# Queries set in halves by transfers, sums added by transfers, reciprocals for two blocks: one hybrid attention block on one core

## The chip, the cores and the metric

One core of a Trainium2 chip runs the whole kernel. Times are device microseconds (us) of one execution. TensorE (PE) multiplies, and its weight loads are listed apart (PEld). VectorE (DVE), ScalarE (ACT) and GpSimd (POOL) work on tiles of 128 partitions. SyncE (SP) and POOL issue transfers (DMAs); a transfer issued by POOL can add what it carries to what is there ("accumulating").

## What is computed

The reference is a decoder block on 16 meta tokens and 512 positions, 1024 channels, all in float32. Cut to what matters here:

```python
proj = h @ w_in                      # h: layer norm of the input; 10 groups of 1024 columns
q_d, k_d, v_d, g_d, q_s, k_s, v_s, g_s, m_d, m_s = split(proj)
# 8 differential heads, two softmaxes each:
s = q @ k.T * 64 ** -0.5 - slope * distance
a = softmax(s0) - lam * softmax(s1);  y_d = rms_norm(a @ v) * 0.8
# 16 stick-breaking heads of 64:
z = q @ k.T * 64 ** -0.5
a = exp(log_sigmoid(z) + sum of log_sigmoid(-z) over later keys);  y_s = a @ v
br_d = (y_d * silu(g_d)) @ w_br_diff;  br_s = (y_s * silu(g_s)) @ w_br_sb
y = (sigmoid(m_d + b) * br_d + sigmoid(m_s + b) * br_s) @ w_out
out = layer_norm(2 ** 0.25 * h + y)
```

## The kernel before, in words

Precision: an operand x of a product is split into a rounded part xh and the rest xl = x - xh, and a product is made of three, xh·yh, xh·yl and xl·yh. Every weight tile (128 x 512) therefore goes through two instructions: ACT rounds it (`hi`, line 174), DVE subtracts (`lo`, line 179).

Order: the work is 16 units (line 69), eight differential heads "d" and eight pairs of stick-breaking heads "s". While unit u's scores and values are worked out, TensorE projects the keys and values of unit u+1 and the queries of unit u+2, and, in "s" units, the two gates. `run` (line 532) mixes the projections with steps that are due at given times. This is the program's order; in the middle section, over all units, the build plans the order on each engine from it, with a model of the durations. `placed` (line 213) ties one instruction behind the one before it on its engine; `keep_order` fixes the order of the start and of the part after the units.

Weights: `items` (line 86) lists the roundings in order, `loads` the transfers that feed them. `fetch` (line 126) asks for a load as soon as a buffer of its ring is free (six "raw", four "rawk", four "rawa"); `prep` (line 183) rounds one item four items ahead of its use. For the eight "s" units keys and values of both halves of the positions are made by seven quarter-size products in place of eight (`stage_kv`, line 633). Of each unit's seven weight operands some are sums of quarters of the weights. a21+a11 and a21+a22 are made by an accumulating transfer from POOL on top of a plain load (`added`, line 148), and two further sums by DVE (`add`, line 153) into a tile `sum`.

Queries (`stage_q`, line 569; the first two heads in `q_hi` and `q_lo`, lines 337 and 341): the projection leaves two heads of 64 rows in one bank. For each head c a tile A[c] holds the rounded query in the head's own 64 partitions and the rest in the other 64. This takes two ACT and two DVE instructions on 64 partitions each:

```python
s.activation(A[c][own], ps[own], AF.Copy, scale=0.125)
v.scalar_tensor_tensor(A[c][oth], ps[own], 0.125, A[c][own], op0=ALU.mult, op1=ALU.subtract)
```

The keys K[c] (line 565) are laid out to match and filled by transfers on SP (`store_k`, line 601).

Differential scores (`d_scores`, line 775) go over four blocks of 128 queries, largest first. After each block's exponentials DVE takes the two reciprocals (line 808), multiplies one by -lambda (809) and combines the two softmaxes (810, 811). The values' sum of squares is split by ACT and POOL (`sqh`, `sql`, line 834) for a product with ones (`ms`, line 841).

Stick-breaking values (`s_values`, line 876): two 64-row halves of a bank `av` must be added. ACT copies one half to `half` (line 889), DVE adds it to the other (line 890) into `ys`. `half` shares one buffer with two tiles of the differential heads. POOL multiplies `ys` by the gate (line 516), and SP stores it (line 518).

Of the kernel before, what the change touches and what calls it, by code (L numbers as in the profile page):

```python
# [16 lines left out]
P = 128  # L17
# [27 lines left out]
def hybrid_block_kernel(ctx: ExitStack, tc: tile.TileContext, x, meta, emb_g, emb_b, w_in, b_gate,  # L45
# [71 lines left out]
    rings = {"raw": (6, []), "rawk": (4, []), "rawa": (4, [])}  # L117
# [8 lines left out]
    def fetch(most=99):  # L126

        for order in (sum_loads, other_loads):
            while order and most:
                l = order[0]  # L130
                src, more, tag = loads[l]
                bufs, log = rings[tag]
                if len(log) >= bufs and left[log[-bufs]] or tag not in pools:
                    break
                raw = pools[tag].tile([P, 4, P], F32, tag=tag, name=tag, bufs=bufs)
                nc.sync.dma_start(raw if l < WOUT else raw.rearrange("p a b -> p (a b)"), src)
                if more is not None:
                    second[l] = lambda raw=raw, more=more: g.dma_start(raw, more, accum_op=ALU.add)
                    if tag == "rawa":
                        added(l)  # L140
                    else:
                        later.append((state["n"] + 3, lambda l=l: added(l)))
                        later.sort(key=lambda x: x[0])
                raws[l] = raw
                log.append(order.pop(0))
                most -= 1

    def added(l):

        if l in second:  # L150
            placed(second.pop(l), ORDERED[3:])
# [14 lines left out]
    def hi(h):  # L166
# [3 lines left out]
        added(item)  # L170
# [165 lines left out]

    def q_hi(n):
        for c, own, _ in HEADS:
            s.activation(A0[n][c][own], pss[n][own], AF.Copy, scale=0.125)

    def q_lo(n):
        for c, own, oth in HEADS:
            a = A0[n][c]
            v.scalar_tensor_tensor(a[oth], pss[n][own], 0.125, a[own].bitcast(F32), op0=ALU.mult, op1=ALU.subtract)
# [199 lines left out]
    with tc.tile_pool(name="att", bufs=1) as ap:  # L544
        pools["sum"] = ap
# [20 lines left out]
        for c, own, oth in HEADS:  # L566
            g.memset(K[c][oth, 1, :].bitcast(F32), 0.0)

        def stage_q(unit, kind, n):
# [12 lines left out]
        def stage_k(unit, kind, n, direct=False):  # L582
# [3 lines left out]
            for m in range(2):  # L586
# [3 lines left out]
                if direct:  # L590
                    for c, own, oth in HEADS:
                        s.copy(K[c][own, 0, o], ps[own])
                        v.tensor_tensor(K[c][own, 1, o], ps[own], K[c][own, 0, o].bitcast(F32), op=ALU.subtract)
                        s.copy(K[c][oth, 0, o], ps[own])
# [6 lines left out]
        def store_k():  # L601

            for o, t in staged:
                for c, own, oth in HEADS:
                    nc.sync.dma_start(K[c][own, :, o].bitcast(F32), t[own].bitcast(F32))
                    nc.sync.dma_start(K[c][oth, 0, o].bitcast(F32), t[own, 0].bitcast(F32))
# [168 lines left out]
        def d_scores(unit, h):  # L775
# [15 lines left out]
            for i in reversed(range(NB)):  # L791
# [15 lines left out]
                r = rz[:, i, :]  # L807
                v.reciprocal(r, zs[:, i, :])
                v.tensor_scalar(r[:, 1:2], r[:, 1:2], nlam, None, op0=ALU.mult)
                v.tensor_scalar(e[0], e[0], r[:, 0:1], None, op0=ALU.mult)  # L810
                v.scalar_tensor_tensor(a[:, AOFF[i]:AOFF[i] + nk], e[1], r[:, 1:2], e[0], op0=ALU.mult, op1=ALU.add)
# [64 lines left out]
        def s_values(unit, c, p, ta):  # L876
# [13 lines left out]
            v.tensor_tensor(unit["y"][own], av[own], half[own], op=ALU.add)  # L890
# [82 lines left out]
    pools["rawa"] = pools["sum"] = lp  # L973
# [228 lines left out]
```

## Time and profile before

| what | value |
|---|---|
| median of three runs | 727.53 us (727.27 to 727.58) |
| the profiled execution | 728.81 us |
| its span, first to last instruction | 727.0 us |
| mean granted TensorE clock | 0.996 |
| instructions | 13330 |

In the profile "a<-b" means that tile a is written from tile b, "x16" counts instructions, and "L890" is line 890 of the kernel. A row of a wait names who waited, for whom, and the total, the count and the longest in us. In a timeline the bracket is the engine's idle time ahead of the instruction and who ended it.

### The profile page before, as it was taken

The page shows a single profiled execution, that of the slowest core. Times are in us where ns is not written, and L with a number is a line of the kernel's source. Part 1 is how long each engine was busy: PE and PEld are TensorE (multiplying, and loading weights), DVE is VectorE, ACT ScalarE, POOL GpSimd, SP SyncE. Part 2 cuts the span into 40 slices and gives each one's busy share as a digit, 9 for nine tenths or more (in the row PEclk, how much of TensorE's full clock was granted, in tenths as well). Part 3 has the DMA queues.
Part 4 walks back from the last instruction along what each step waited for, and adds up shares of the span by engine and source line. Part 5 has one row for each costly group of instructions (what it writes and reads, how often), then busy time and mean ns, then how long its engine had stood idle before and what let it go on. Part 6 is the DMA issues. An engine that isn't in the chain of part 4 may idle for free.

```text
span 727.0 us, 13330 instructions
## 1 busy us (share of the span) xinstructions
PE 713.1 (98%) x4594; PEld 649.6 (89%) x4594; DVE 585.6 (81%) x1246; ACT 428.8 (59%) x1023; POOL 111.7 (15%) x133
## 2 busy tenths in 40 slices
PE   9999999999999999999999999999999999999994
PEld 8999999999999888898989898988888998999783
DVE  6887668678998889797968797968395888778787
ACT  5675666666787776575756575655365455555300
POOL 3210141011012000130202000001012202130002
PEclk9999999999999999999999999999999999999998
DMA  8343448343346644647645443583258748696802
GB/s 292 97 140 101 126 121 146 101 133 102 109 102 149 156 132 124 152 106 185 139 139 130 121 119 102 177 259 102 59 143 162 146 119 184 137 182 189 302 20 101
DMA packets 153798, 101.86 MB, mean 140 GB/s; under 512 B 7249, under 2 KB 141810, under 8 KB 153730
## 3 DMA queue, kind: packets, MB, share of 16 engines
q1 hardware_dynamic: 135650, 89.99, 42.6%
q0 software_dynamic: 17760, 9.96, 10.7%
q10 hardware_dynamic: 320, 1.06, 0.4%
q8 instruction: 36, 0.59, 0.3%
q14 instruction: 32, 0.26, 0.1%
HBM read 79.38 MB, written 7.86 MB: 120 GB/s over the span
## 4 chain that ended last, share of the span: by engine, by line
PE 82%; DMA 6%; DVE 6%; ACT 3%; issue 1%; POOL 1%; SPq 0%; DVEq 0%; POOLq 0%; ACTq 0%
PE ps L500 12%; PE ps L484 11%; PE ps L486 11%; PE ps L485 11%; PE q L1009 10%; PE q L651 10%; PE sc L717 5%; PE t L723 3%; DMA raw<-in_w_out_dram 2%; PE t L728 1%; PE bank L375 1%; DMA ysT<-gs 1%; PE av L885 1%; PE tv L684 1%; PE av L886 1%
## 5 line engine op out<-in xcount | busy, mean ns | idle before, releaser
L179 DVE TENSOR_TENSOR wl<-raw,wh 128x512 fp32r<-128x512 f32 x172 | 119.0, 697 | 34.6 <-ACT wh L174 33.0
L485 PE MATMUL ps<-hTl,wh 128*128 128x512 f32 x368 | 145.6, 396 | 0.0
L484 PE MATMUL ps<-hTh,wh 128*128 128x512 f32 x368 | 145.3, 395 | 0.2 <-DVE kvt L668 0.2
L486 PE MATMUL ps<-hTh,wl 128*128 128x512 f32 x368 | 144.5, 393 | 0.0
L174 ACT CAST wh<-raw 128x512 fp32r<-128x512 f32 x172 | 105.5, 622 | 34.0 <-PE ps L485 20.2
L486 PEld LDWEIGHTS ps<-hTh,wl 128*128 128x128 f32 x368 | 69.2, 188 | 13.5
L484 PEld LDWEIGHTS ps<-hTh,wh 128*128 128x128 f32 x368 | 69.2, 188 | 13.2 <-DVE kvt L668 0.4
L485 PEld LDWEIGHTS ps<-hTl,wh 128*128 128x128 f32 x368 | 69.2, 188 | 12.4
L500 PE MATMUL ps<-hTh,wh 128*128 128x264 f32 x256 | 73.5, 287 | 0.0
L500 PE MATMUL ps<-hTl,wh 128*128 128x264 f32 x256 | 73.4, 287 | 0.0
L500 PE MATMUL ps<-hTh,wl 128*128 128x264 f32 x256 | 73.2, 286 | 0.0
L717 PE MATMUL sc<-k,A 128*128 128x264 f32 (+3 forms) x320 | 66.6, 297 | 0.5 <-DMA k<-ks 0.3
L734 DVE TENSOR_TENSOR al<-t,ah 128x512 fp32r<-128x512 f32 (+2 forms) x88 | 45.6, 526 | 25.2 <-ACT ah L733 19.4
L1009 PE MATMUL q<-gh,wl 128*128 128x256 f32 x224 | 63.8, 285 | 0.0
L1009 PE MATMUL q<-gl,wh 128*128 128x256 f32 x224 | 63.6, 284 | 0.0
L1009 PE MATMUL q<-gh,wh 128*128 128x256 f32 x224 | 63.1, 282 | 0.2 <-ACT t L1018 0.2
L733 ACT CAST ah<-t 128x512 fp32r<-128x512 f32 (+2 forms) x88 | 40.2, 465 | 34.5 <-PE t L723 26.3
L871 DVE TENSOR_TENSOR_SCAN e<-e,diag 128x528 f32<-128x528 f32 (+1 forms) x64 | 54.6, 858 | 4.9 <-ACT e L865 4.6
L717 PEld LDWEIGHTS sc<-k,A 128*128 128x128 f32 x320 | 50.4, 189 | 4.1 <-issue 0.7
L500 PEld LDWEIGHTS ps<-hTh,wl 128*128 128x128 f32 x256 | 48.3, 189 | 0.5
L500 PEld LDWEIGHTS ps<-hTl,wh 128*128 128x128 f32 x256 | 48.3, 189 | 0.5
L500 PEld LDWEIGHTS ps<-hTh,wh 128*128 128x128 f32 x256 | 48.3, 188 | 0.4
(274 smaller groups left out, 1764.6 us busy)
## 6 DMA issues: line engine op xcount, KB each, us to landing
raw<-in_w_in_dram SPq DMA_DIRECT2D x144, 256.0 KB, 3.2
k<-ks SPq DMA_DIRECT2D x60, 132.0 KB, 2.7
rawk<-in_w_in_dram SPq DMA_DIRECT2D x16, 256.0 KB, 3.4
rawk<-in_w_in_dram POOLq DMA_DIRECT2D x16, 256.0 KB, 6.5
raw<-in_w_out_dram SPq DMA_DIRECT2D x16, 256.0 KB, 3.5
k<-ks SPq DMA_DIRECT2D x60, 66.0 KB, 2.3
raw<-in_w_br_diff_dram SPq DMA_DIRECT2D x12, 256.0 KB, 3.7
raw<-in_w_br_sb_dram SPq DMA_DIRECT2D x12, 256.0 KB, 3.5
```

The costliest lines, as they stand in the source:

```text
L174: s.copy(wh, raw)
L179: eng.tensor_tensor(wl, raw, wh.bitcast(F32), op=ALU.subtract)
L484: pe.matmul(ps, wh[:, k % 4, :], hTh[:, k, M:], start=(k == 0), stop=False)
L485: pe.matmul(ps, wh[:, k % 4, :], hTl[:, k, M:], start=False, stop=False)
L486: pe.matmul(ps, wl[:, k % 4, :], hTh[:, k, M:], start=False, stop=(k == KT - 1))
L500: pe.matmul(ps[:, :H2], a[:, k % 4, :], b[:, k, ts(c, H2)], start=(k == 0 and m == 0), stop=(k == KT - 1 and m == 2))
L651: pe.matmul(bank, a[:, k, :], b, start=start and k == 0 and j == 0, stop=k == 3 and j == 2, skip_group_check=not start)
L717: pe.matmul(ps[:, :n], q, K[:, m, k0:k0 + n], start=(m == 0), stop=(m == 1))
L733: s.copy(h, t[:, o:o + w])
L734: v.tensor_tensor(l, t[:, o:o + w], h.bitcast(F32), op=ALU.subtract)
L871: v.tensor_tensor_scan(rev, rev, diag[0][:, L - nk:][:, ::-1], 0.0, ALU.mult, ALU.max)
L1009: pe.matmul(bank, a[:, k, :], b[:, n, k, :], start=start and k == 0 and m == 0, stop=k == 3 and m == 2, skip_group_check=not start)
```

## The change

- `stage_q`: ACT rounds both heads at once on 128 partitions into A[0], DVE subtracts both at once into a new tile `low`, and three transfers on SP set the halves in their places. `q_hi` and `q_lo` keep two instructions each, with other partitions. The rest now stands in partitions 64 to 127 for both heads, and the keys' layout follows.
- Weights of the "s" units: the sum a21+a22+a11 is loaded once and added to twice by transfers; a21+a22 gets a load and an accumulation of its own. One DVE addition per unit stays, made in place. The ring "rawk" has five buffers, and the tile `sum` of the middle section goes.
- `d_scores`: reciprocals, the multiplication by -lambda and the combination are made for two blocks after every second block.
- `s_values`: ACT copies both halves, and an accumulating transfer from POOL adds one to the other in `y`.

```diff
-            loads += [(a11, None, "raw"), (a21, a11, ring), (a21, a22, ring), (a12, None, "raw"), (a22, None, "raw")]
-            items += [o, o + 1, (o + 2, o), o + 3, o + 2, o + 4, (None, o + 3)]
+            if ring == "rawa":
...
+            else:
+                loads += [(a11, None, "raw"), (a21, (a11,), ring), (a21, (a22, a11), ring), (a12, None, "raw"),
+                          (a21, (a22,), ring), (a22, None, "raw")]
+                items += [o, o + 1, o + 2, o + 3, o + 4, o + 5, (o + 2, o + 3)]
...
-    rings = {"raw": (6, []), "rawk": (4, []), "rawa": (4, [])}
+    rings = {"raw": (6, []), "rawk": (5, []), "rawa": (4, [])}
...
-                    second[l] = lambda raw=raw, more=more: g.dma_start(raw, more, accum_op=ALU.add)
+                    second[l] = [lambda raw=raw, x=x: g.dma_start(raw, x, accum_op=ALU.add) for x in more]
                     if tag == "rawa":
                         added(l)
                     else:
-                        later.append((state["n"] + 3, lambda l=l: added(l)))
+                        for n in range(len(more)):
+                            later.append((state["n"] + 3 + 3 * n, lambda l=l: added(l)))
...
-        for l in items[h]:
-            added(l)
         one = sums.pop(True) if first is None else raws[first]
-        raw = one if first is None else pools["sum"].tile([P, 4, P], F32, tag="sum", name="sum", bufs=1)
+        raw = one
+        if first is not None and loads[first][2] == "rawa":
+            raw = lp.tile([P, 4, P], F32, tag="sum", name="sum", bufs=1)
         v.tensor_tensor(raw, one, raws[other], op=ALU.add)
...
     def q_hi(n):
-        for c, own, _ in HEADS:
-            s.activation(A0[n][c][own], pss[n][own], AF.Copy, scale=0.125)
+        s.activation(A0[n][0], pss[n], AF.Copy, scale=0.125)
+        s.activation(A0[n][1][LO], pss[n][HI], AF.Copy, scale=0.125)
...
-            for c, own, oth in ((0, LO, HI), (1, HI, LO)):
-                s.activation(A[c][own], ps[own], AF.Copy, scale=0.125)
-                v.scalar_tensor_tensor(A[c][oth], ps[own], 0.125, A[c][own].bitcast(F32), op0=ALU.mult,
-                                       op1=ALU.subtract)
+            low = gpool.tile([P, S], F32R, tag="sg", name="low")
+            s.activation(A[0], ps, AF.Copy, scale=0.125)
+            v.scalar_tensor_tensor(low, ps, 0.125, A[0].bitcast(F32), op0=ALU.mult, op1=ALU.subtract)
+            for o, src in ((A[1][LO], A[0][HI]), (A[1][HI], low[HI]), (A[0][HI], low[LO])):
+                nc.sync.dma_start(o.bitcast(F32), src.bitcast(F32))
...
-                for c, own, oth in HEADS:
-                    nc.sync.dma_start(K[c][own, :, o].bitcast(F32), t[own].bitcast(F32))
-                    nc.sync.dma_start(K[c][oth, 0, o].bitcast(F32), t[own, 0].bitcast(F32))
+                for c, own, _ in HEADS:
+                    nc.sync.dma_start(K[c][LO, :, o].bitcast(F32), t[own].bitcast(F32))
+                    nc.sync.dma_start(K[c][HI, 0, o].bitcast(F32), t[own, 0].bitcast(F32))
...
-                r = rz[:, i, :]
-                v.reciprocal(r, zs[:, i, :])
...
+                if i % 2 == 0:
+                    r = rz[:, i:i + 2, :]
+                    v.reciprocal(r, zs[:, i:i + 2, :])
+                    v.tensor_scalar(r[:, :, 1:2], r[:, :, 1:2], nlam, None, op0=ALU.mult)
+                    for i in (i + 1, i):
...
             s.copy(half[own], av[oth])
-            v.tensor_tensor(unit["y"][own], av[own], half[own], op=ALU.add)
+            s.copy(unit["y"][own], av[own])
+            placed(lambda: g.dma_start(unit["y"][own], half[own], accum_op=ALU.add), ORDERED[3:])
```

## Rows read from the trace of the kernel before

**Rows 1.** The page: the span and each engine's busy time.
```profile
span 727.0 us, 13330 instructions
PE 713.1 (98%) x4594; PEld 649.6 (89%) x4594; DVE 585.6 (81%) x1246; ACT 428.8 (59%) x1023; POOL 111.7 (15%) x133
```

**Rows 2.** The chain: shares by engine; two pieces (start us, us, what).
```profile
PE 82%; DMA 6%; DVE 6%; ACT 3%; issue 1%; POOL 1%; SPq 0%; DVEq 0%; POOLq 0%; ACTq 0%
...
384.22 2.70 PE q L651 x22
...
557.64 40.32 PE q L1009 x336
```

**Rows 3.** Waits of TensorE's weight loads, 220 to 320 us, seven rows.
```profile
PEld av L882 <- DVE a L754: 0.5, 1, 0.5
...
PEld q L651 <- DVE ks L658: 0.3, 1, 0.3
```

**Rows 4.** Busy time by stretch: stretch, its length, engines, granted clock, DMA share.
```profile
core 0: us, PE busy (x) PEld busy (x) DVE busy (x) ACT busy (x) POOL busy (x), PEclk, DMA share, GB/s
261.00:285.00 24.00, 23.61 (x165) 21.82 (x164) 23.67 (x42) 18.17 (x50) 1.28 (x1) 1.00 0.42 125
381.00:417.00 36.00, 36.00 (x230) 32.52 (x228) 30.42 (x55) 22.50 (x57) 5.14 (x4) 1.00 0.50 125
```

**Rows 5.** Groups by line and shape: total busy us, mean ns of one | idle before.
```profile
L577 DVE SCALAR_TENSOR_TENSOR A<-ps,A 64x512 fp32r<-64x512 f32 x28 | 19.3, 689 | 2.2 <-ACT A L576 1.5
L576 ACT ACTIVATE A<-ps 64x512 fp32r<-64x512 f32 x28 | 16.5, 590 | 9.1 <-DVE A L577 8.9
L514 DVE TENSOR_TENSOR sg<-ps,sg 128x512 f32<-128x512 f32 x16 | 10.7, 678 | 0.0
L160 DVE TENSOR_TENSOR sum<-rawk,raw 128x512 f32<-128x512 f32 x8 | 5.5, 685 | 3.7 <-DMA raw<-in_w_in_dram 3.7
L890 DVE TENSOR_TENSOR ys<-av,half 64x512 f32<-64x512 f32 x14 | 9.6, 688 | 0.2
L808 DVE RECIPROCAL rz<-zs 128x2 f32<-128x2 f32 x32 | 5.2, 161 | 7.8 <-ACT e L804 7.4
L809 DVE TENSOR_SCALAR rz<-rz,nlam 128x1 f32<-128x1 f32 x32 | 6.8, 212 | 0.8
```

**Rows 6.** SP's transfers (KB each, us to landing), SP's waits, one of ACT's.
```profile
k<-ks SPq DMA_DIRECT2D x60, 132.0 KB, 2.7
...
SPq L136 <- DVE wl L179: 245.7, 86, 12.3
...
SPq L518 <- POOL ys L516: 25.7, 7, 4.7
...
ACT wh L174 <- DMA raw<-in_w_in_dram: 1.0, 1, 1.0
```

**Rows 7.** POOL's accumulating transfers (L138): issue ns min/median/max, landing, one wait.
```profile
L138 POOL DMA_DIRECT2D rawk<-in_w_in_dram x16: 1269/1418/2927, 104.4 to 385.5; - x16
...
DMA to landing us min/median/max: 4.3/5.8/11.1
...
POOL rawk L138 <- DMA rawk<-in_w_in_dram: 5.7, 1, 5.7
```

**Rows 8.** ACT in order of time: start us, us, line, operation.
```profile
305.98 0.58 ACT L889 COPY half<-av 64x512 f32<-64x512 f32 x1 [0.52 <-PE av L887]
...
308.46 0.40 ACT L662 COPY kvt<-q 128x264 f32<-128x264 f32 x1
...
407.19 0.58 ACT L889 COPY half<-av 64x512 f32<-64x512 f32 x1 [1.15 <-PE av L887]
...
417.50 0.58 ACT L889 COPY half<-av 64x512 f32<-64x512 f32 x1 [0.67 <-PE av L887]
```

**Rows 9.** POOL and PE in order of time: the rest `sql` and its product.
```profile
223.84 1.29 POOL L834 TENSOR_TENSOR sql<-sq,sqh 128x512 fp32r<-128x512 f32 x1 [10.68 <-ACT sqh L833]
...
228.57 0.39 PE L841 MATMUL ms<-sql,onesm 128*128 128x512 f32 x1
```

More of the change, by code (lines that the diff above doesn't have):

```diff
@@ L95, in hybrid_block_kernel @@
             o = len(loads)
-            loads += [(a11, None, "raw"), (a21, a11, ring), (a21, a22, ring), (a12, None, "raw"), (a22, None, "raw")]
-            items += [o, o + 1, (o + 2, o), o + 3, o + 2, o + 4, (None, o + 3)]
+            if ring == "rawa":
+                loads += [(a11, None, "raw"), (a21, (a11,), ring), (a21, (a22,), ring), (a12, None, "raw"), (a22, None, "raw")]
+                items += [o, o + 1, (o + 2, o), o + 3, o + 2, o + 4, (None, o + 3)]
+            else:
+                loads += [(a11, None, "raw"), (a21, (a11,), ring), (a21, (a22, a11), ring), (a12, None, "raw"),
+                          (a21, (a22,), ring), (a22, None, "raw")]
+                items += [o, o + 1, o + 2, o + 3, o + 4, o + 5, (o + 2, o + 3)]
         elif n < 4:
@@ L148, in added @@
     def added(l):
-        if l in second:
-            placed(second.pop(l), ORDERED[3:])
+        if second.get(l):
+            placed(second[l].pop(0), ORDERED[3:])
     def add(h):
         first, other = items[h]
-        for l in items[h]:
-            added(l)
         one = sums.pop(True) if first is None else raws[first]
-        raw = one if first is None else pools["sum"].tile([P, 4, P], F32, tag="sum", name="sum", bufs=1)
+        raw = one
+        if first is not None and loads[first][2] == "rawa":
+            raw = lp.tile([P, 4, P], F32, tag="sum", name="sum", bufs=1)
         v.tensor_tensor(raw, one, raws[other], op=ALU.add)
@@ L169, in hi @@
         item = items[h]
-        added(item)
+        assert not second.get(item)
         raw = raw0[:, h // 2, ts(h % 2, 4)] if item is None else sums.pop(h) if isinstance(item, tuple) else raws[item]
@@ L337, in q_hi @@
     def q_hi(n):
-        for c, own, _ in HEADS:
-            s.activation(A0[n][c][own], pss[n][own], AF.Copy, scale=0.125)
+        s.activation(A0[n][0], pss[n], AF.Copy, scale=0.125)
+        s.activation(A0[n][1][LO], pss[n][HI], AF.Copy, scale=0.125)
     def q_lo(n):
-        for c, own, oth in HEADS:
-            a = A0[n][c]
-            v.scalar_tensor_tensor(a[oth], pss[n][own], 0.125, a[own].bitcast(F32), op0=ALU.mult, op1=ALU.subtract)
+        for c, own, _ in reversed(HEADS):
+            v.scalar_tensor_tensor(A0[n][c][HI], pss[n][own], 0.125, A0[n][0][own].bitcast(F32), op0=ALU.mult,
+                                   op1=ALU.subtract)
     def banks(*of):
@@ L544, in hybrid_block_kernel @@
     with tc.tile_pool(name="att", bufs=1) as ap:
-        pools["sum"] = ap
         apads = []
@@ L565, in hybrid_block_kernel @@
         K = [ap.tile([P, 2, L], F32R, name=f"k{c}") for c in range(2)]
-        for c, own, oth in HEADS:
-            g.memset(K[c][oth, 1, :].bitcast(F32), 0.0)
+        for c in range(2):
+            g.memset(K[c][HI, 1, :].bitcast(F32), 0.0)
         def stage_q(unit, kind, n):
@@ L590, in stage_k @@
                 if direct:
[L591 to L594, printed above, removed]
+                    s.copy(K[0][LO, 0, o], ps[LO])
+                    v.tensor_tensor(K[0][LO, 1, o], ps[LO], K[0][LO, 0, o].bitcast(F32), op=ALU.subtract)
+                    s.copy(K[0][HI, 0, o], ps[LO])
+                    s.copy(K[1][HI, 0, o], ps[HI])
+                    v.tensor_tensor(K[1][LO, 1, o], ps[HI], K[1][HI, 0, o].bitcast(F32), op=ALU.subtract)
+                    s.copy(K[1][LO, 0, o], ps[HI])
                     continue
@@ L603, in store_k @@
             for o, t in staged:
-                for c, own, oth in HEADS:
-                    nc.sync.dma_start(K[c][own, :, o].bitcast(F32), t[own].bitcast(F32))
-                    nc.sync.dma_start(K[c][oth, 0, o].bitcast(F32), t[own, 0].bitcast(F32))
+                for c, own, _ in HEADS:
+                    nc.sync.dma_start(K[c][LO, :, o].bitcast(F32), t[own].bitcast(F32))
+                    nc.sync.dma_start(K[c][HI, 0, o].bitcast(F32), t[own, 0].bitcast(F32))
             staged.clear()
@@ L806, in d_scores @@
                         yield
-                r = rz[:, i, :]
-                v.reciprocal(r, zs[:, i, :])
-                v.tensor_scalar(r[:, 1:2], r[:, 1:2], nlam, None, op0=ALU.mult)
-                v.tensor_scalar(e[0], e[0], r[:, 0:1], None, op0=ALU.mult)
-                v.scalar_tensor_tensor(a[:, AOFF[i]:AOFF[i] + nk], e[1], r[:, 1:2], e[0], op0=ALU.mult, op1=ALU.add)
+                if i % 2 == 0:
[3 more added lines that the diff above has]
+                    for i in (i + 1, i):
+                        nk = NKEY[i]
+                        e = [E[c][:, ZOFF[i]:ZOFF[i] + nk] for c in range(2)]
+                        v.tensor_scalar(e[0], e[0], rz[:, i, 0:1], None, op0=ALU.mult)
+                        v.scalar_tensor_tensor(a[:, AOFF[i]:AOFF[i] + nk], e[1], rz[:, i, 1:2], e[0], op0=ALU.mult,
+                                               op1=ALU.add)
                 yield
@@ L972, in hybrid_block_kernel @@
     lr = ctx.enter_context(tc.tile_pool(name="later", bufs=2))
-    pools["rawa"] = pools["sum"] = lp
+    pools["rawa"] = lp
     LEFT, RIGHT = ts(0, 256), ts(1, 256)
```

## The prediction

> **What bounds the kernel now.** I read the page first, then the chain, the waits of TensorE's weight loads, and the busy times by stretch. The page gives TensorE 713.1 of 727.0 us, DVE 585.6, ACT 428.8, POOL 111.7 [rows 1]. A busy TensorE need not be at its peak, so I looked for its pace. In the chain 336 products of 256 columns take 40.32 us, 120 ns each, one behind the other, and 22 of 264 columns in the middle of the kernel 2.70 us, 123 ns each; the chain as a whole is 82% TensorE [rows 2]. So TensorE's queue is full nearly throughout, and the change alters no product. What can be won is the time in which that queue stands. The waits show where. Between 220 and 320 us seven weight loads stand until DVE or ACT is ready; the first and the last of the seven rows are shown, and their sum is 0.5 + 4 x 0.4 + 2 x 0.3 = 2.7 us [rows 3]. Outside it the same view has only waits of the start and of the last third, where the change alters little. The stretch is the changeover from the last differential head to the first two stick-breaking units. There DVE is busy 23.67 of 24 us, while in a later unit it has 30.42 of 36; the granted clock is 1.00 in both, its upper level of 2.4 GHz [rows 4]. DVE is the bound for a moment, TensorE for the rest.
>
> **The change, part by part.**
>
> *Queries by transfers.* Of the 14 heads that go through the stage, each drops one of two DVE instructions (689 ns) and one of two ACT instructions (590 ns). The two that are left work on 128 partitions in place of 64. The trace has a 128-partition DVE instruction on the same kind of source, 678 ns, so height costs nothing here [rows 5]. DVE: 14 x 0.689 = 9.6 us less. ACT: 14 x 0.59 = 8.3 us less. Three transfers of 64 partitions come in on SP's queue: 42 issues. The nearest row is the key transfers, 132 KB from 64 partitions to 64, landing in 2.7 us [rows 6]. The third overwrites what the first and DVE's subtraction read, so SP must stand for the first's landing, 2.7 us a head. Behind it in SP's queue are weight loads, stores and key transfers. Their cover: SP already stands 245.7 us in all for weight buffers to come free, because it runs far ahead [rows 6]; ACT's first rounding waits for a weight load only 1.0 us in the whole run [rows 6]. The queries themselves are used a whole unit later (a stick-breaking one is 36 us long). Cost taken: nothing; if the cover were gone, up to 2.7 us a head.
>
> *Quarters' sums.* In each of eight units one of two DVE additions goes, 685 ns: 5.5 us less [rows 5]. In its place come one more load on SP and two more accumulating transfers on POOL, 16 in all. Each holds POOL 1.27 to 2.93 us and lands 4.3 to 11.1 us after issue, 5.8 at the median [rows 7]. The buffers are asked for a unit or more ahead, so nothing on TensorE's path waits for them as long as POOL's queue moves. The memory is neutral: one more weight buffer, one sum buffer less.
>
> *Stick-breaking halves.* Sixteen times DVE's addition of two halves (688 ns) becomes an ACT copy and an accumulating transfer on POOL. DVE: 11.0 us less [rows 5]. ACT: 16 x 0.58 = 9.3 us more [rows 8]. Behind the transfer waits the multiplication by the gate, on POOL; behind that a store on SP, which stands up to 4.7 us there already [rows 6] and will stand a landing longer, 4 to 6 us. The store's reader is the last unit's reload, so it costs nothing until then.
>
> *Reciprocals for two blocks.* 16 reciprocals and 16 small multiplications go: 16 x (0.161 + 0.212) = 6.0 us of DVE [rows 5]. The weights of one block are ready later, by one block's work; the transposes that read them come after the last block in any case.
>
> *Start and new key layout.* Same instruction counts, other partitions; nothing.
>
> **The sum.** DVE loses 9.6 + 5.5 + 11.0 + 6.0 = 32.1 us of 585.6, ACT gains 1.0. In one stick-breaking unit DVE loses 0.69 + 0.69 + 2 x 0.69 = 2.75 us. Each DVE wait of the changeover is at most 0.5 us, so 2.75 us a unit is several times what each needs. Six of the seven are DVE's: 2.7 - 0.4 = 2.3 us. The seventh is ACT's, at 308.46 us: the copy `kvt` comes 2.5 us after a copy `half`, with ACT busy in between [rows 8]. The new copy, 0.58 us, stands in that same line, so this wait grows to 1.0 us. Bounds: every wait gone, -2.7; none gone and the new copy exposed in full at its row, +0.6; I take the removal, because DVE's relief is large beside the waits: -2.3 + 0.6 = -1.7 us. The profiled execution took 728.81 us, 1.8 outside its span of 727.0; the median of the runs is 727.53, 1.28 lower. The difference is put on the median: **725.8 us**. A difference under 0.2%, 1.46 us, can't be told from none here: 726.07 is the edge, and my number lies just beyond it.
>
> **A rule against the change.** The rows first: four accumulating transfers issued in one bunch hold POOL up to 2.93 us and land up to 11.1 us later; a lone one 1.27 us [rows 7]. The Trainium skill (SBUF — State Buffer, "SBUF: two separate sides") says that descriptors of POOL-issued transfers are written by GpSimd, which is shut out of the port it shares with DVE while DVE runs an instruction that takes both ports, and advises issuing from SP or ACT. By that rule the 32 new transfers would all behave like the slow ones, which is the third rival below; by the lone rows they cost nothing.
>
> **Rivals.**
> 1. *The waits move* (0.24). The middle section's order of instructions is planned when the kernel is built, and a changed program gets a changed order. The seven waits may go and others of 0.3 to 0.5 us come. For: nothing in a unit of 36 us leaves TensorE idle, so any slip shows. Against: DVE has more slack than before. Time: between three waits fewer and three more at 0.5 us, the longest of the seven, 726.0 to 729.0; middle 727.5.
> 2. *POOL blocked, slower* (0.15). The second accumulation into a buffer must wait in POOL's queue for the first to land. What stands behind it on POOL is `sql`, and TensorE's second product of `ms` waits for `sql`. Near 224 us `sql` ends at 225.13 and its product starts at 228.57: 3.4 us of slack [rows 9]. A second accumulation just ahead of it costs a landing, 5.8, and an issue, 1.4 [rows 7]: 7.2 - 3.4 = 3.8 us. For: POOL has stood 5.7 us for such a landing in that place already [rows 7]. Against: `sql` comes once a unit and takes 1.29 us, and the second is asked for three rounding steps after the first. It decides once the stand is over 3.4 us. Time: 727.5 + 3.8 = 731.3 once, 735.1 twice. The Trainium skill (DMA: Bandwidth & Descriptors, "Two DMAs through the same engine are not ordered") says the issuing engine has to wait for the first transfer's semaphore; the stand is therefore certain, only its neighbour isn't.
> 3. *The buffer of the halves, slower* (0.07). It is one buffer. Two copies into it stand 10.3 us apart (407.19 and 417.50) [rows 8]. The transfer now holds it: 1.2 us of copies plus landing. At a landing of 4.3 to 5.8 us that is 5.5 to 7.0; at 11.1 it is 12.3, and ACT would stand 2.0 us with TensorE's copies behind it, over some seven units: 14 us, 741.5. It decides at a landing of 9.1 us.
> 4. *Relief that isn't used* is part of the first: if the waits of the changeover come from the order and not from DVE's load, the change does what it says and the time stays.
>
> **How the numbers follow.** The forecast has 0.54, with its own range 724.5 (every wait gone, -2.7, and the 0.3 us by which the runs shown scatter) to 727.0 (half of DVE's waits staying, -1.15, and the copy exposed, +0.6); about three quarters of it lie beyond the edge. Faster: 0.40. Same: 0.14 of the forecast and 0.24 of the first rival, 0.38. Slower: 0.15 + 0.07 = 0.22. The range reaches from 724.5 to one blocked `sql`, 731.3; what is left out is a second block, the halves' buffer, and more gain than the waits hold.
>
> **What would show it.** Right: DVE near 553 us busy, ACT near 430, TensorE's busy time about 2 us less with the same count of products, no weight load waiting for DVE between 230 and 310 us, and ACT's `kvt` among the few left. The first rival: such waits at other places, their sum still near 3 us. The second: POOL waiting for a `rawk` landing, with a wait of `ms` for `sql` on TensorE. The third: ACT's `half` or `ys` waiting for a transfer. I am wrong altogether if TensorE's pace itself changes, or if weight loads come late behind SP's stands.

## The result, and the profile after

The changed kernel takes 730.12 us (728.75 to 732.69), against 727.40 for the kernel before on the same chip: a ratio of 1.0034 [1.0021, 1.0048], slower by about 2.5 us. The forecast was 725.8, faster. The profiled execution took 730.05 us, its span is 728.1. The page's busy times, software queue and chain answer to [rows 1, 2]:

```profile
PE 710.9 (98%) x4594; PEld 649.0 (89%) x4594; DVE 561.2 (77%) x1176; ACT 428.8 (59%) x1025; POOL 144.7 (20%) x165
...
q0 software_dynamic: 27488, 16.26, 17.9%
...
PE 85%; DVE 5%; DMA 4%; ACT 3%; POOL 1%; issue 1%; SPq 1%; DVEq 0%; POOLq 0%; ACTq 0%
```

DVE is 24.4 us less busy and TensorE 2.2 us, with the same 4594 products. Most of DVE's relief came, and yet the end comes later. Busy time by stretch (the columns as in [rows 4]) shows that DVE is no longer full where the forecast looked, but nearly so elsewhere, from 240 to 250 us:

```profile
220.00:320.00 100.00, 98.08 (x629) 88.79 (x627) 80.99 (x153) 70.57 (x175) 28.94 (x27) 1.00 0.79 176
261.00:285.00 24.00, 24.00 (x163) 22.12 (x162) 19.48 (x37) 16.84 (x44) 3.85 (x4) 1.00 0.55 136
...
240.00:250.00 10.00, 8.81 (x65) 8.19 (x65) 9.29 (x16) 7.11 (x16) 4.00 (x5) 1.00 1.13 230
```

In 261 to 285 us DVE had 23.67 of 24 us to do and now has 19.48; TensorE is busy throughout. So the seven waits of [rows 3] are gone, the one for `kvt`, which was to grow, among them. What came is in the same view, the waits of TensorE's weight loads, first from 190 to 260 us, then from 470 to 490:

```profile
PEld q L660 <- DVE vT L680: 2.3, 2, 1.4
PEld ps L491 <- ACT vT L625: 1.0, 1, 1.0
...
PEld sc L726 <- issue: 2.2, 1, 2.2
```

Four stands (that for `vT` is 0.9 us at 220 us and 1.4 at 244), 2.3 + 1.0 + 2.2 = 5.5 us, where 3.4 us stood: the seven small ones of 2.7 us, and one of 0.7 us in the same view of the kernel before, at 483 us:

```profile
PEld sc L717 <- issue: 0.7, 1, 0.7
```

That is 2.1 us more: 0.6 in the changeover and 1.5 at the last unit's scores. The two traces agree: the first product behind the units starts 2.05 us later (before and after, PE in order of time):

```profile
557.48 0.28 PE L1009 MATMUL q<-gh,wh 128*128 128x256 f32 x1
...
559.53 0.28 PE L1024 MATMUL q<-gh,wh 128*128 128x256 f32 x1
```

The medians differ by 2.7 us and the two profiled executions by 1.24, since that of the kernel before lies 1.4 us above its median. The stand at the last unit's scores is seen by the products too; two pairs of them, before and after:

```profile
480.68 0.41 PE L717 MATMUL sc<-k,A 128*128 128x264 f32 x2
483.91 0.48 PE L717 MATMUL sc<-k,A 128*128 128x264 f32 x2 [0.30 <-DMA k<-ks]
...
481.09 0.41 PE L726 MATMUL sc<-k,A 128*128 128x264 f32 x2
483.49 0.49 PE L726 MATMUL sc<-k,A 128*128 128x264 f32 x2 [1.98 <-DMA k<-ks]
```

The keys let the second pair go at nearly the same time in both. But in the kernel before eleven other products stand between the pairs, and in the changed plan none, so TensorE asks for these keys some 2 us sooner than they come. Why they come so late stands on SP, in the timeline of its queue, after and then before:

```profile
469.03 2.99 SPq L967 DMA_DIRECT2D ydT<-gd  x6
472.12 0.53 SPq L967 DMA_DIRECT2D ysT<-gs  x1
...
475.07 0.63 SPq L614 DMA_DIRECT2D k<-ks  x1
...
479.12 0.48 SPq L615 DMA_DIRECT2D k<-ks  x1
...
474.26 2.61 SPq L952 DMA_DIRECT2D ysT<-gs  x4
...
479.17 1.28 SPq L605 DMA_DIRECT2D k<-ks  x2
```

In both kernels the last unit's keys go out behind reloads of 256 KB that nobody needs yet. The stands at 220 and 244 us are shown by DVE's timeline ahead of the first, and by ACT's waits from 220 to 250 us ahead of the second:

```profile
219.66 0.83 DVE L823 TENSOR_SCALAR e<-e,rz 128x528 f32<-128x528 f32 x2
220.40 0.77 DVE L824 SCALAR_TENSOR_TENSOR apad<-e,rz,e 128x528 f32<-128x528 f32 x1
221.08 0.42 DVE L680 TENSOR_TENSOR vT<-kvt,q 128x264 f32<-128x264 f32 x1
```

```profile
ACT wh L180 <- DMA rawk<-in_w_in_dram: 2.3, 1, 2.3
```

At 220 us the combination of two blocks, which the change put together, stands ahead of the copy `vT` for which TensorE waits. And ACT waits 2.3 us for a weight buffer `rawk` that POOL is still adding to; the forecast had said that nothing on TensorE's path would wait for these. Neither slower rival came in the form in which it was told: no weight load waits for `sql`, no copy for the buffer `half`.

### The profile page after: what moved, and what is told of

It is laid out like the page before. It is cut to its first block, busy times and chain, and to the rows that moved or that the text cites. A ratio compares the mean times of both kernels' runs of the same rounds, so it can differ in the third digit from the quotient of the medians.

```text
span 728.1 us, 13424 instructions
## 1 busy us (share of the span) xinstructions
PE 710.9 (98%) x4594; PEld 649.0 (89%) x4594; DVE 561.2 (77%) x1176; ACT 428.8 (59%) x1025; POOL 144.7 (20%) x165
## 4 chain that ended last, share of the span: by engine, by line
PE 85%; DVE 5%; DMA 4%; ACT 3%; POOL 1%; issue 1%; SPq 1%; DVEq 0%; POOLq 0%; ACTq 0%
PE ps L507 12%; PE ps L491 11%; PE ps L493 11%; PE ps L492 11%; PE q L660 11%; PE q L1024 10%; PE sc L726 5%; PE t L732 3%; PE t L737 1%; DMA hr<-in_x_dram 1%; PE bank L382 1%; PE av L899 1%; PE av L900 1%; PE tv L693 1%; DVE hr L1174 1%
## 5 line engine op out<-in xcount | busy, mean ns | idle before, releaser
L185 DVE TENSOR_TENSOR wl<-raw,wh 128x512 fp32r<-128x512 f32 x172 | 121.4, 711 | 44.3 <-ACT wh L180 42.9
L493 PEld LDWEIGHTS ps<-hTh,wl 128*128 128x128 f32 x368 | 69.2, 188 | 13.4
L143 POOL DMA_DIRECT2D rawk<-in_w_in_dram x32 | 42.3, 1699 | 50.6 <-DMA rawk<-in_w_in_dram 34.1
```

Of the source, the lines that this page charges most:

```text
L143: second[l] = [lambda raw=raw, x=x: g.dma_start(raw, x, accum_op=ALU.add) for x in more]
L185: eng.tensor_tensor(wl, raw, wh.bitcast(F32), op=ALU.subtract)
L493: pe.matmul(ps, wl[:, k % 4, :], hTh[:, k, M:], start=False, stop=(k == KT - 1))
```

## Experiments

All are timed over five rounds beside the kernel before. The first four expectations name their theories by number, the later ones by letter.

**One part at a time.** Each kernel has one part's lines of the diff above on the kernel before: queries with the key layout, quarters' sums with their ring and the `sum` tile, halves, reciprocals.

```diff
+ q_only: q_hi, q_lo, K's memset, stage_q, stage_k, store_k as changed
+ s_only: loads, items, rings, later, added, add as changed
+ h_only: s.copy(unit["y"][own], av[own]); g.dma_start(unit["y"][own], half[own], accum_op=ALU.add)
+ r_only: reciprocal, -lambda and combination for two blocks after every second
```

> The kernel before with the queries' halves by transfers alone. Theory 1 (the order that is planned at the build sets the waits; any edit deals them anew): some other set of TensorE waits of 0.3 to 2 us, time within 2 us of before on either side, and the single parts don't add up to the +2.7 us of the whole. Theory 2 (the sums by transfers load the queues and come late): no loss here, 726 to 728 us, no wait of over 1 us at the last unit's scores near 481. Theory 3 (SP stands for the queries' low part, and the key transfers behind it come late): the wait for keys near 481, 2 us, is here, 729 to 730 us.

> The kernel before with the three quarters' sums by transfers alone. Theory 1: some other set of waits, within 2 us of before. Theory 2: this part carries the loss: ACT's rounding waits 2 us for an accumulated weight near 230, TensorE 1.3 us for vT near 244, the keys of the last unit are late; 729 to 730 us. Theory 3: no loss, 726 to 728 us.

> The kernel before with the stick-breaking halves added by transfers alone. Theory 1: another set of waits, within 2 us of before. Theories 2 and 3: DVE's relief of 1.4 us a unit takes away part of the changeover's waits, 725.5 to 727.5 us, no wait near 481 above 0.5 us.

> The kernel before with the reciprocals of two blocks at once alone. Theory 1: another set of waits, within 2 us of before. A fourth theory (the two blocks' combinations come in one burst of 2 us on DVE and hold up vT): a wait of TensorE for vT of 0.9 us near 220, 728 to 728.5 us. Theories 2 and 3: 726.5 to 727.5 us.

| part alone | ratio to before | DVE busy, us | TensorE's stands that are new or larger |
|---|---|---|---|
| queries | 1.0050 [1.0033, 1.0068] | 576.0 | 0.5 to 1.6 us, 217 to 246 us; lower clock behind them |
| quarters' sums | 1.0020 [1.0010, 1.0031] | 582.7 | 1.9 at 237 us, five of 0.5 to 0.9 |
| halves | 0.9992 [0.9982, 1.0003] | 577.9 | 1.2 at 241 us, two of 0.8; none near 483 |
| reciprocals | 0.9980 [0.9968, 0.9991] | 581.1 | none above 0.6 |

DVE's relief adds up, 9.6 + 2.9 + 7.7 + 4.5 = 24.7 us. Near 481 us no part stands longer than the kernel before, and the stand behind two blocks' combination isn't in the reciprocals alone. So the whole kernel's stands are not the parts' stands put together, and theories 3 and 4 fall for the single parts. Of theory 2 there is a part: in the sums alone ACT waits 1.3 us for `rawk`, and they lose 1.4 us. Theory 1 has the places right, but its bound of 2 us fails for the queries, which lose 3.6; and the reciprocals' 727.06 us is also what theories 2 and 3 gave. The queries alone, waits of the weight loads from 200 to 260 us, of DVE from 240 to 247, of SP from 216 to 232, and then the busy times from 220 to 230:

```profile
PEld q L654 <- DVE low L577: 1.6, 1, 1.6
PEld sc L720 <- DVE mn L803: 1.5, 2, 0.8
PEld q L654 <- DVE vT L674: 1.0, 1, 1.0
...
DVE sum L160 <- DMA raw<-in_w_in_dram: 2.0, 1, 2.0
...
SPq L579 <- DVE low L577: 8.2, 1, 8.2
```

```profile
220.00:230.00 10.00, 9.09 (x50) 7.99 (x49) 8.39 (x26) 6.05 (x18) 2.53 (x2) 0.83 0.14 32
```

SP stood 8.2 us for DVE's `low`, with weight loads and key transfers behind it, and a little later DVE stood 2.0 us for a weight load. The granted clock is 0.83 of full speed over these ten microseconds, just behind three of TensorE's stands (0.5 to 0.8 us, 218 to 221 us), so part of them ran at the lower of its two levels, 1.2 GHz; it is 1.00 there in the kernel before. By estimate that is 10 x 0.17 = 1.7 us of TensorE's full pace.

**The late keys.** Only SP's order differs from the changed kernel: `follow` ties each reload behind the last key transfer.

```diff
+ state["stored"] = [i for i in nc.cur_bb.bb.instructions[-30:] if i.engine == mybir.EngineType.SP][-1]   # end of store_k
...
  nc.sync.dma_start(y[j], kept[of][j])
+ follow(new, state["stored"])    # new: the reload just issued
```

> The changed kernel with one thing altered: on SP's queue the 14 reloads of gated and ungated outputs for the last unit come behind the last unit's key transfers instead of ahead of them. The order on TensorE, DVE, ACT and POOL is the changed kernel's. Theory A (late keys at the end): the 2.14 us in which TensorE stood near 481 us go, the rest stays; 728.0 us against the changed kernel's 730.1, ratio to before near 1.0005. Rival B (that wait is covered: the last unit is bound by something behind it, and TensorE stands somewhere else by as much): 730 us, with a new wait of about 2 us after 484 us, most likely for the reloads themselves.

Measured: 727.62 us, ratio 0.9998 [0.9987, 1.0009], 0.0036 less than the changed kernel: 2.6 us for a stand of 2.2. Theory A holds. The keys now go out at 471.76 to 475.6 us, ahead of the reloads, and no wait is left at 481; the stands of the changeover stay as they were:

```profile
PEld q L661 <- DVE vT L681: 2.3, 2, 1.4
PEld ps L491 <- ACT vT L626: 1.0, 1, 1.0
PEld ms L856 <- POOL sql L849: 0.3, 1, 0.3
```

**Earlier accumulations.** Only POOL's order differs from the changed kernel.

```diff
-                            later.append((state["n"] + 3 + 3 * n, lambda l=l: added(l)))
+                            later.append((state["n"] + 2 + 2 * n, lambda l=l: added(l)))
```

> The changed kernel with the accumulating transfers of the quarters' sums asked for earlier: 2 and 4 rounding steps after the first load in place of 3 and 6. Only POOL's order differs. Theory C (the 2.3 us in which ACT stood for an accumulated weight buffer near 230 us is what TensorE's 1.35 us at 244 us, and perhaps part of the 0.9 at 220, come from): ACT's wait for that buffer goes, TensorE stands about 1.3 us less between 240 and 250 us, 728.8 us, ratio to before near 1.0015. Rival D (TensorE's waits of the changeover come from where the order puts DVE's transposed copies behind other DVE work, not from the buffer): ACT's wait goes, TensorE's stay within 0.5 us, 730 us. Rival E (earlier accumulations hold POOL): sql or bias late, over 731.

Measured: 731.14 us, ratio 1.0043 [1.0029, 1.0056]. ACT's wait for `rawk` is gone, but both of TensorE's stands behind `vT` are there in full, so theory C falls and D holds: ACT's stand wasn't what TensorE waited for. In the changed kernel DVE shows no idle time from 238 us on, and the copy `vT` has its turn at 244.99. Instead a new wait came, E's, and it is the second rival of the prediction, POOL's accumulations ahead of `sql` (waits from 195 to 260 us; the stand near 481 us was 0.8 in this kernel):

```profile
PEld q L660 <- DVE vT L680: 2.3, 2, 1.4
PEld ms L855 <- POOL sql L848: 1.8, 1, 1.8
```

**Without the queries, and a change of plan with no change of work.** The first has the other three parts. The second is the kernel before with one number of the plan altered, the pace at which a differential head's score blocks are asked for.

```diff
+ no_q: s_only + h_only + r_only
...
-TD = (0.85, 11.0, 14.5)
+TD = (0.9, 11.0, 14.5)     # due_c
```

> The change without its queries and key layout: quarters' sums, halves and reciprocals alone. Theory F (each part's cost adds to the others'): +1.4 for the sums, -0.2 for the halves, -1.6 for the reciprocals, -0.4 us in all against the kernel before: 728.2 where before is 728.6, ratio 0.9995. Theory G (each combination gets its own planned order and so its own waits, which do not add): anything between 0.997 and 1.005, with waits on TensorE at other places than in the single parts; a ratio of 1.003 or more would say that the queries carry no loss of their own.

> The kernel before with no work changed: only the pace at which a differential head's ten score blocks are asked for is 0.90 in place of 0.85 in the plan, which gives TensorE, DVE and ACT another order in the middle section. Theory G (a changed plan alone moves the time by as much as the parts of the change do): TensorE's seven waits of the changeover are replaced by others, the time moves by 1 us or more either way, ratio outside 0.9985 to 1.0015. Rival H (the plan is robust, and the losses come from what the change adds): ratio within 0.9985 to 1.0015, waits of TensorE between 220 and 320 us summing to 2 to 3.5 us.

Three parts that sum to -0.4 us cost 1.0045 [1.0029, 1.0061], +3.3 us: theory F falls. And the kernel before, with no work changed, comes to 1.0096 [1.0082, 1.0111], 7 us slower, more than any part. The four largest of its waits from 195 to 320 us:

```profile
PEld ps L484 <- DVE kvt L668: 2.4, 1, 2.4
PEld av L819 <- DVE yd L851: 1.3, 1, 1.3
PEld t L723 <- ACT A L576: 1.1, 1, 1.1
PEld q L651 <- DVE vT L671: 0.9, 2, 0.7
```

So the order that the build plans is worth more than all the waits that the change could have removed, 2.7 us.

**TensorE held to another kernel's order.** Here each of TensorE's instructions is tied behind the one that came before it in the other kernel's plan (the list is written into the file); the other engines order themselves around that. In the two kernels with queries two buffers had to be set apart as well.

```diff
+ for one, two in zip(order, order[1:]):
+     tc.add_manual_dep(two, one.name, NoSync)
...
-            low = gpool.tile([P, S], F32R, tag="sg", name="low")
+            low = gpool.tile([P, S], F32R, tag="low", name="low", bufs=1)     # after_border5, q_border
...
-    rings = {"raw": (6, []), ...
+    rings = {"raw": (5, []), ...
```

> The whole change, with TensorE's instructions held in the order that they have in the kernel before (all 4,525 in the same place). Two sizes differ with it: the query's low part has a buffer of its own, and the ring of weight loads has 5 buffers in place of 6. DVE, ACT, POOL and SP order themselves around that. Theory G (the loss is TensorE's changed order, and the work that the change takes off DVE is worth what was forecast): TensorE waits for DVE at the changeover for less than 1.5 us in all, 726.5 against 728.1 before, ratio 0.996 to 0.999. Rival I (the change's own transfers and additions carry the loss, whatever the order): 729.5 or more, ratio 1.002 or more, with TensorE's waits between 200 and 250 us led back to A, rawk, or SP's and POOL's queues. Rival J (the order as planned suits the work it was planned with; a foreign order costs by itself): over 731.

> The kernel before, no work changed, with TensorE's instructions held in the order that they have in the changed kernel. Theory G: the changed kernel's waits come with its order: TensorE stands at the same four places (200, 220, 244 and 481 us) for 4 us or more, ratio 1.003 to 1.006 (730.3 to 732.5). Rival I (the loss is the change's own transfers): waits at the old places only, ratio within 0.9985 to 1.0015. Rival J: any foreign order costs, over 1.006, with waits at places that neither kernel has.

> Quarters' sums, halves and reciprocals, without the queries, with TensorE's instructions held in the order of the kernel before; no buffer differs. The same parts in their own planned order came to 1.0045 [1.0029, 1.0061]. Theory G: the 2.5 us go, and DVE's 22.5 us less take most of the 2.3 us of waits at the changeover: 726 to 727.5, ratio 0.997 to 0.999. Rival I: 729.5 or more, ratio 1.002 or more, with ACT or DVE waiting for rawk between 220 and 300 us.

> The queries and the key layout alone, with TensorE's instructions held in the order of the kernel before; the query's low part has a buffer of its own and the ring of weight loads 5 buffers in place of 6. In its own planned order this part came to 1.005 [1.0033, 1.0068]. Theory G: ratio 0.997 to 1.000, DVE's waits at the changeover smaller by half. Rival K (SP's stands for the queries delay the weight loads and key transfers behind them, which the order does not cure): ratio 1.002 or more, with DVE or ACT waiting for raw or k near 230 to 250 us, as in this part's own order.

| kernel | TensorE's order | ratio to before |
|---|---|---|
| after_border5 | before's | 1.0165 [1.0143, 1.0188] |
| before_aorder | after's | 1.0066 [1.0042, 1.0090] |
| no_q_border | before's | 1.0039 [1.0024, 1.0054] |
| q_border | before's | 1.0110 [1.0095, 1.0125] |

Theory G, that the order of before would bring the forecast gain, falls. Part of the loss is most likely the experiment's own doing: both kernels with a ring of five weight buffers stand 2.7 to 3.0 us in the last third (after_border5 here, from 655 to 680 us), where no kernel with six stands over 1.2 us at once, and the granted clock of both is 0.97 from 640 to 700 us. The ring was not run by itself.

```profile
PEld q L1024 <- ACT t L1029: 3.0, 1, 3.0
```

Their totals say nothing of the change; their changeovers do. In after_border5, the whole change, the waits from 195 to 320 us add up to 4.2 us, and the last unit's scores stand 0.7 as in the kernel before. In q_border they add up to 2.2 us, none above 0.9: in this order the queries cost nothing there, and rival K falls. In no_q_border, where no buffer was altered, TensorE's waits of that stretch and ACT's from 225 to 235 us are

```profile
PEld t L733 <- ACT r L856: 2.8, 1, 2.8
PEld q L656 <- ACT kvt L667: 1.3, 1, 1.3
PEld av L892 <- DVE a L759: 1.1, 1, 1.1
PEld av L896 <- DVE al L739: 0.3, 1, 0.3
...
ACT wh L180 <- DMA rawk<-in_w_in_dram: 3.2, 1, 3.2
```

5.5 us in place of 2.7. DVE's own fell from about 2.3 to 1.4, as forecast in direction, `kvt` rose as forecast (to 1.3; I had said 1.0), and 2.8 us stand behind one accumulated buffer: rival I for the sums. Last, before_aorder shows an order meeting work that it was not planned for. The place is one of the changed kernel's four, 244 us, as theory G has it, but the stand for `vT` is 3.9 us there in place of 1.4, the other three are 0.2 us or less (the last keys just come in time there), and the interval holds rival J's bound of 1.006: the two can't be told apart by it. The clock is 0.83 from 240 to 260 us (waits from 195 to 320 us, then the busy times of that stretch):

```profile
PEld q L651 <- DVE vT L671: 4.2, 2, 3.9
```

```profile
240.00:260.00 20.00, 16.27 (x86) 14.63 (x85) 12.84 (x23) 12.63 (x27) 1.29 (x1) 0.83 0.43 123
```

**The first two units' quarters as before, in the same order.** For these two units one accumulation into each of two buffers and DVE's two additions come back, with the ring of four and the `sum` tile; the other six units keep the new way.

```diff
-            if ring == "rawa":
+            if ring == "rawa" or i in (0, 1):
...
-    rings = {"raw": (6, []), "rawk": (5, []), "rawa": (4, [])}
+    rings = {"raw": (6, []), "rawk": (4, []), "rawa": (4, [])}
```

> Sums, halves and reciprocals with TensorE held in the order of the kernel before, as in no_q_border, but the first two stick-breaking units' quarters are added as before (one accumulating transfer, two additions on DVE, ring of 4 buffers and a sum buffer); the other six units keep the new way. Theory L (the sums' cost is the third quarter buffer of the second unit, which the ring of 5 lets in late, because a unit now takes three buffers in place of two): ACT's 3.2 us of waiting for rawk at 231 us and TensorE's 2.7 behind it go; the waits of 1.1 near 281 and 1.3 near 310 stay; 728.2 against 730.8 of no_q_border, ratio to before 1.000 to 1.001. Rival M (TensorE's stand at 231 has another cause, ACT's order or DVE's, and the buffer only came last): it stays over 1.5 us; ratio 1.003 or more.

Measured: 732.75 us, 1.0080 [1.0064, 1.0095]; the total of theory L was missed, most likely by the experiment's own ring. The stand at 231 us went, as theory L says, and M, which had it stay, falls. But the next unit, the first of the new way, now draws on four buffers, and there ACT waits longer (its waits from 255 to 310 us, TensorE's from 195 to 320):

```profile
ACT wh L182 <- DMA rawk<-in_w_in_dram: 8.7, 2, 7.6
...
PEld av L898 <- ACT ah L741: 3.6, 1, 3.6
```

Five buffers, 3.2 us at the second unit; four, 7.6 at the third. A unit of the new way takes three of these buffers where the old took two, so five last 5/3 = 1.7 units where four lasted 4/2 = 2, and the late buffer moves with the ring. This is a cost of the sums themselves. That the ring's length brings it is argued: the order of the loads on SP and of the accumulations on POOL changed with it, and a ring of six was not tried.

**The same pair under two other plans.**

```diff
-TD = (0.85, 11.0, 14.5)
+TD = (0.8, 11.0, 14.5)     # due_f on before, after_f on the changed kernel; after_c has 0.9
```

> The kernel before with no work changed, score blocks asked for every 0.80 in the plan in place of 0.85. Theory G2 (the plan of before is an unusually good one for its work; nearly any other costs): slower than before, ratio 1.002 to 1.010, with new waits between 200 and 320 us. Rival H2 (0.90 was a bad plan and others are as good as before's): ratio within 0.9985 to 1.0015.

> The changed kernel with the plan's pace 0.90 in place of 0.85; its pair is due_c at 1.0096 to before. Theory G2 (the change's work is worth its 1.7 us, its own plan at 0.85 was only not as lucky as before's): it beats its pair by 1 to 5 us, ratio to before 1.002 to 1.008. Rival N (the change's work itself costs 2 to 3 us, in any plan): slower than its pair, ratio over 1.012.

> The changed kernel with the plan's pace 0.80; its pair is due_f. Theory G2: faster than its pair by 1 us or more. Rival N: slower than its pair by 2 us or more. Equal within 1 us would say that the change's gain and its cost balance and that the sign of its result is the plan's.

| plan's pace | work of before | changed work |
|---|---|---|
| 0.85 | 1 | 1.0034 [1.0021, 1.0048] |
| 0.90 | 1.0096 [1.0082, 1.0111] | 1.0014 [1.0002, 1.0026] |
| 0.80 | 1.0022 [1.0007, 1.0038] | 1.0013 [1.0005, 1.0022] |

The sign of the change's result is the plan's. At 0.90 the changed work is 6 us faster than its pair (the ratios differ by 0.0082; 1 to 5 us were expected), at 0.85 it is 2.5 us slower, at 0.80 the two can't be told apart. Rival N, that the changed work costs in any plan, falls. For the work of before its own plan, 0.85, is the best of the three.

**Two versions put together.** The first is the changed kernel at pace 0.80 with the keys first, as above; the second has reciprocals and halves alone, with the keys first.

```diff
+ after_f_keys: TD = (0.8, 11.0, 14.5); follow(new, state["stored"])
+ rh_keys: r_only + h_only; follow(new, state["stored"])
```

> The changed kernel in the plan with pace 0.80 (1.0013 [1.0005, 1.0022] to before), with the 14 reloads of the last unit behind its key transfers on SP, as in after_keys; only SP's order differs. Theory A: the 1.25 us in which TensorE stood for keys near 480 us go and nothing comes in their place: 727.0 us, ratio 0.999 to 1.000. Rival B: 728.2, the wait moves behind 484 us.

> Reciprocals and halves alone, in their own plan, with the last unit's reloads behind its key transfers on SP. Theory F (parts that add no chain of transfers in front of TensorE keep their gains): -1.6 for the reciprocals, -0.2 for the halves, -0.3 for the keys: ratio 0.9965 to 0.9985, 726 us. Theory G (each plan has its own waits): outside of that, with one or more waits of over 1 us between 200 and 320 us; over 1.002 if the plan is as poor as that of sums, halves and reciprocals together.

Measured: 0.9984 [0.9972, 0.9997] and 0.9985 [0.9973, 0.9997], 727.10 and 727.33 us against 728.08. Both beat the kernel before by 1 us, and after_f_keys has the whole change in it: theory A again, the wait of 1.3 us at 480 gone. Its waits from 100 to 520 us are

```profile
PEld q L661 <- DVE vT L681: 1.5, 1, 1.5
PEld q L661 <- DVE vT L683: 0.4, 1, 0.4
PEld q L661 <- DVE tl L640: 0.2, 1, 0.2
PEld t L733 <- issue: 0.2, 1, 0.2
```

2.3 us, less than before's. Halves and reciprocals together keep about what the reciprocals gave alone (0.9980); these three versions can't be told apart. For rh_keys the sum of the parts, theory F, holds at the edge of its range, with no stand over 0.8 us in the changeover; G has no support there.

## Why the prediction was wrong

*What bounds the kernel* was right: the pace of TensorE's products, with only its stands to win. Stands of 5.5 us after against 3.4 before account for the 2.05 us between the two traces. The sign "TensorE's busy time about 2 us less" came true in a slower kernel, by luck: it says nothing of the end.

*The price of DVE's relief* was read from the wrong end. "Six of the seven are DVE's", -2.3 us, went as told. The step that failed is the one after it, that nothing takes their place because "DVE's relief is large beside the waits": 1.0 us of waits was to be left in the changeover, and 3.3 stood there. The relief is in DVE's sum, but TensorE waits for one copy at one moment, and when that copy comes is a matter of the order. DVE has 19 us to spare from 220 to 320 us, and TensorE still stood 0.9 and 1.4 us for `vT`. I had this as the first rival at 0.24, with waits "of 0.3 to 0.5 us" and 729.0 as its far end. Its mechanism was right, and so was its sum "near 3 us"; the single stands are longer, 0.9 to 1.4 us. With the last unit's keys put first the kernel comes to 727.62 us, in the middle of that rival. How long a plan's stands are is not bounded by the old plan's: one number altered, with no work changed, cost 7 us.

*Quarters' sums, nothing* was wrong. "The buffers are asked for a unit or more ahead, so nothing on TensorE's path waits for them as long as POOL's queue moves": POOL's queue moved, but I counted the buffers and not how many a unit takes. ACT waited 1.3 us for one in the sums alone, 2.3 in the changed kernel, 3.2 in no_q_border. In the changed kernel itself that wait was covered, as after_early showed; in no_q_border the stand behind it was TensorE's largest.

*Queries, nothing, "if the cover were gone, up to 2.7 us a head"*: the cover is the plan's. In the order of before the changeover lost nothing by them; in their own plan SP stood 8.2 us for DVE, three times my bound, since I had priced the stand for the first transfer's landing and not the one for DVE's `low`.

*Halves*: the multiplication and store behind the landing cost TensorE nothing, as told, and the buffer `half` held up no copy. The wait for `kvt`, which was to grow to 1.0 us by the new copy, is not in the changed kernel. *Reciprocals*: "the transposes come after the last block in any case" is right, but DVE's two combinations now come in one piece, and in this plan the copy `vT` came behind them.

*DVE's 32.1 us* came out at 24.4. Instructions in a row start closer together than they last (in the timeline above the second starts 0.68 us before the third but lasts 0.77), so a mean from the group view is more than the busy time that goes with it. And other work stretched: the 172 subtractions `wl`, untouched by the change, take 711 ns at the mean in place of 697, 2.4 us. The price of the time did not hang on it.

*The rule against the change* (the Trainium skill, SBUF — State Buffer, "SBUF: two separate sides") was rightly left out of the sum as a certainty. No run here bears it out. Of the 32 `rawk` issues of the changed kernel those that stand alone hold POOL 1.27 to 1.33 us, as the lone ones before; only those right behind other work of POOL, the later ones of a bunch above all, take longer, up to 3.47. TensorE waits for none of them. The 1.8 us in after_early came by the order of POOL's queue, as in the second rival, with issues of 1.27 us ahead of `sql`.

*The last unit's keys* are the second step that failed, and the one that made the kernel slower. "Outside it the same view has only waits of the start and of the last third, where the change alters little" passed over the 0.7 us at 483 us, the longest wait of that view behind the start: it belongs to the last unit, whose order the change plans anew. It was put at nothing and grew by 1.5 us; with the keys first the loss of 2.5 us was gone (0.9998). I had read SP's queue for what the change adds to it, and not for who else in it is near to being late.

What stays open: why the plan of before is so good for its work. The plans were compared with each other, not with a model of the chip, and without the ordering rule for the keys a plan for the changed work as good as that one was for its own was not found.

## What to carry to other kernels

Where the build plans the order, an edit is also a new plan, and a planned kernel's time scatters by several us over plans that do the same work. Before an edit worth less than that is judged, plan it and the kernel before twice more with a number nudged, and compare pairs; then look for the few largest stands and tie those down, which gave 2.6 us here at the cost of one ordering rule. A short wait in the old trace is a place where the new plan may ask sooner. When an edit makes a unit take more buffers of a ring, count the units that the ring lasts, not the buffers.

## What was not expected of the hardware

The granted clock can fall behind short stands: 0.83 over 20 us behind one of 3.9 us in before_aorder, 0.91 in the same stretch of due_c behind several of 0.7 to 2.4, while the changed kernel's 2.2 us at 481 left it at 1.00 (470 to 490 us). The length of the stand doesn't settle it: behind q_border's 2.7 us it is 0.97 (640 to 700 us), and behind no_q_border's 2.8 it stays at 1.00 (220 to 245 us). Where it falls, a stand costs more than its length.

Small transfers land later here with large ones ahead of them. Issued between 466 and 484 us, the key transfers of 132 and 66 KB landed in 4.6 and 5.2 us (median) behind the reloads, and in 3.0 and 2.2 ahead of them:

```profile
k<-ks SPq DMA_DIRECT2D x4, 132.0 KB, 4.6
k<-ks SPq DMA_DIRECT2D x4, 66.0 KB, 5.2
```

That is the changed kernel; with the keys first the same two lines of the transfers' view read

```profile
k<-ks SPq DMA_DIRECT2D x4, 132.0 KB, 3.0
k<-ks SPq DMA_DIRECT2D x4, 66.0 KB, 2.2
```
